# Attention steps of a hybrid decoder moved by one or two products between the matrix products

## The chip, the cores and the metric

The kernel runs on one core of one Trainium2 chip. A core has five engines that run at the same time, each with its own queue that is worked off in order: TensorE (PE in the profile; its weight loads are shown apart as PEld), VectorE (DVE), ScalarE (ACT), GpSimd (POOL) and SyncE (SP), and DMA queues that move data between memory and the on-chip buffers. Engines wait for each other with semaphores. The metric is the time of one execution on the device in microseconds (us).

## The reference

The program computes one inference step of a four-layer decoder, cut here to two layers, on 1024 prompt tokens and 8 decode tokens, all with D_MODEL = 2048, in float32. Layer A mixes by pooling and a gate, then projects out. After it, one shared pair of keys and values is projected. Layer B is sliding-window attention with a learned sink per head:

```python
def attn_core(q, k, v, q_pos, k_pos, sinks):
    s = jnp.einsum('...qkgd,...skd->...kgqs', q, k).astype(jnp.float32) * (HEAD_DIM ** -0.5)
    ...
    s = jnp.where(mask[..., None, None, :, :], s, NEG)
    sink = sinks.astype(jnp.float32).reshape(N_KV_HEADS, GROUP)[:, :, None, None]
    m = jnp.maximum(jnp.max(s, axis=-1, keepdims=True), sink)
    p = jnp.exp(s - m)
    p = p / (jnp.sum(p, axis=-1, keepdims=True) + jnp.exp(sink - m))
    return jnp.einsum('...kgqs,...skd->...qkgd', p.astype(v.dtype), v)
```

Around it stand two large products: `z = x @ w_in` gives queries and gate, and `(o * silu(gate)) @ w_out` goes into a LayerNorm with the residual. There are 32 heads of 64 channels, 4 key heads, and a window of 128 positions.

## The kernel before

**Products.** Nearly all of TensorE's time is large matrix products. The tokens are cut into two chunks of 512 and 520. A product block of 2 by 2 is computed with Strassen's seven products instead of eight (`seven`, `pair`): each of the seven takes one weight block of 128 x 1024, which ScalarE rounds to a high part (`cast_to`, line 475) and VectorE completes by the rest (`prep_to`, line 490), and 24 matmuls of 256 or 260 columns: high times high, high times low, low times high (lines 654 to 656). In this document a *product* is one of these groups of 24 matmuls, and a *slot* is one product with what is issued around it.

**The order of the work** is written out by hand. `begin` opens a slot: it first issues what the product before left over (`flush`), then the loads, casts and subtractions of weights some products ahead. Then come the 24 matmuls. `end` closes the slot: it issues on TensorE what was entered with `self.product(n, rank, go)` for this slot, lower rank first, and then what was entered with `self.at(n, go)` for it; n counts slots from where the entry is made. So everything entered in a slot stands in an engine's queue behind the weight work of that slot and ahead of the left-over work of the next. `in_order` keeps this order on TensorE, VectorE and ScalarE.

**The left-over work of the seven products** moves partial sums between three accumulator banks called a, b, c. The products run in the order 0, 2, 1, 5, 3, 4, 6; I call their places 0 to 6. After place 0 ScalarE writes the negative of bank a into bank b (line 593), and the product at place 2 adds to bank b. After place 2 ScalarE copies bank b out (line 602), before the product at place 4 adds to it. After place 4 ScalarE copies bank b into bank a (line 614), before the product at place 6 adds to it. Lines 599, 608 and 627 are further copies by ScalarE, and lines 615 and 620 subtractions by VectorE.

**The attention stage** (phase `bi`) makes, per pair p of query tiles, seven products for the queries (places 0 to 6, slots 0 to 6) and seven for the gates (slots 7 to 13). When a query pair is done, SyncE moves a rotated copy (line 1612), and VectorE applies the rotary embedding at the end of slot 10 with three large operations (two at line 1620, one at line 1728): the *rope*. Then each of the two query tiles t of the pair goes through the steps of `attend`, entered in slots counted from the start of the pair:

- `score`: TensorE writes scores to the accumulator tile S (line 1758)
- `select`: ScalarE copies the older half of the window (line 1775)
- `largest`: VectorE puts in the newer half and takes the maximum (lines 1779 to 1787)
- `expo(0)`, `expo(1)`: ScalarE exponentials of four heads' blocks each, with sums (lines 1792, 1794)
- `total`: VectorE adds the sink's part and inverts (lines 1801, 1802)
- `norm(0)`, `norm(1)`: ScalarE scales four blocks each (line 1807)
- `turn`: TensorE transposes into the first half of S (line 1811)
- `keep`: ScalarE copies the transposes (line 1820), then VectorE writes a masked copy of them (line 1821)
- `values`: TensorE multiplies by the values (line 1835)
- `gate`: VectorE multiplies by the gate (line 1844); in chunk 0 every second tile adds four sums and differences (lines 822 to 825)

The two tiles of a pair start seven slots apart, so with `at` = 11 + 7n each step always meets the same place of the seven. A gate's tanh (line 1873) follows the last product of the gates. Large buffers come from one set of 53 (`Mem`), and the one that has been free longest is taken next; in phase `bi` of chunk 1 the distance at which weights are prepared drops from 3 to 2 products where fewer than 4 are free. In chunk 0 the first four pairs run as plain products with a different step, and only pairs 4 to 7 run as sevens; there VectorE also makes four sums of weight blocks per seven products (line 333) for chunk 1. Chunk 1 runs all eight pairs as sevens, and in pairs 4 and 7 with steps of the decode tokens in between (`decode`).

Of the kernel before, what the change touches and what calls it, by code (L numbers as in the profile page):

```python
# [74 lines left out]
X_AGE = 3  # L75
SIDE_KEEP = 5

DEC_AT = (0, 1, 6, 6, 7, 8, 9, 10, 13, 13), (11, 11, 12, 12, 13, 14, 15, 16, 17, 17)


# [101 lines left out]
class Kern:  # L182
# [1556 lines left out]
        self.at(0, a)  # L1739
        self.at(lag, b)  # L1740

    def attend(self, c, t, at, s1, s2, late=False):


        nc = self.nc
# [43 lines left out]
        def expo(n):  # L1789
            mx, nm, es, rs = x["sm"]  # L1790
            if n == 0:
                nc.scalar.activation(es[:], es[:], AF.Exp)
            for i in range(4 * n, 4 * n + 4):
                nc.scalar.activation(  # L1794
                    x["s3"][:, i, :], x["s3"][:, i, :], AF.Exp, bias=nm[:, i : i + 1], scale=0.125,
                    accum_out=rs[:, i : i + 1],
                )
# [6 lines left out]
        def norm(n):  # L1804
            rs = x["sm"][3]
            for i in range(4 * n, 4 * n + 4):
                nc.scalar.activation(x["s3"][:, i, :], x["s3"][:, i, :], AF.Copy, scale=rs[:, i : i + 1])
# [48 lines left out]
                z.free()  # L1856

        self.product(at, 2, score)
        for n, go in enumerate((
            select, largest, lambda: expo(0), lambda: expo(1), total, lambda: norm(0), lambda: norm(1)  # L1860
        )):
            self.at(at + 1 + n, go)
        self.product(at + s1, 0, turn)
        self.at(at + s1 + 1, keep)
        self.product(at + s1 + s2, 1, values)
# [32 lines left out]
    def decode(self, c, pr):  # L1898
# [86 lines left out]

        for n, go in zip(DEC_AT[pr], (s0, s1, s2, s3, s4, s5, s6, s7, s8, s9)):
            if go in (s0, s2, s6, s8):
# [6 lines left out]
    def phase_bi(self, c, ps, nxt):  # L1994
        nc = self.nc
        T = CHUNKS[c][1]
        if ps[0] == 0:
            self.kv_open(c)
        if not self.strassen:
            for done in (self.k_done, self.v_done):  # L2000
                box = {}
                for j in range(2):

                    def take(ps, j=j, done=done, box=box):
                        if j == 0:
                            box["s"] = self.mem.full()
                        nc.scalar.copy(box["s"].a[:, j * T : (j + 1) * T], ps[:])
                        if j == 1:
                            done(c, box["s"])

                    self.unit(take)
            for t in range(2 * ps[0], 2 * ps[-1] + 2):
                def q_done(ps, t=t):
                    s = self.mem.half()
                    nc.scalar.copy(s.a[:, :T], ps[:])
                    self.q_done(c, t, s, 1, 4)

                def g_done(ps, t=t):
                    s = self.mem.half()
                    nc.scalar.copy(s.a[:, :T], ps[:])  # L2020
                    self.gate_done(c, t, s, 1)

                self.attend(c, t, 9, 13 if t <= 2 * ps[-1] else 8, 2)
                self.unit(q_done)
                if t == 2 * ps[-1] - 1:
                    self.x_begin(nxt)
                self.last = t == 2 * ps[-1] + 1
                self.unit(g_done)
            self.last = False
            return  # L2030
        if ps[0] == 0:
            pairs = []
            for done in (self.k_done, self.v_done):
                box, z0, z1 = self.two(T)
                pairs.append((z0, z1, lambda done=done, box=box: done(c, box["s"])))
            self.both(c, *pairs)

        def queries(p):
            t0 = 2 * p
            if T > TP and p % 4 == 3:  # L2040
                self.at(2, lambda p=p: self.dec_keys(p // 4))
            for n in range(2):
                t = t0 + n
                self.attend(c, t, 11 + 7 * n, {13: 10, 14: 10, 15: 8}.get(t, 12), 2, t > 12)
            if p == ps[-1]:
                self.x_begin(nxt)
                if c == 1:
                    self.ahead = 6, 3, 2
            box, z0, z1 = self.two(T)
            self.pair(c, z0, z1, lambda t0=t0, box=box: self.q_done(c, t0, box["s"], 2, 3))  # L2050

        def gates(p):
            box, z0, z1 = self.two(T)

            def done():
                self.gate_done(c, 2 * p, box["s"], 2)
                if T > TP and p % 4 == 3:
                    self.decode(c, p // 4)

            self.last = p == ps[-1]  # L2060
            self.pair(c, z0, z1, done)

        for p in ps:
            queries(p)
            gates(p)
        self.last = False
# [260 lines left out]
```

## Time and profile before

| what | value |
|---|---|
| median of 3 runs | 2356.72 us (2354.07 to 2358.65) |
| profiled execution | 2351.39 us |
| its span, first to last instruction | 2349.6 us |
| TensorE busy with matmuls | 2303.9 us, 98% |
| VectorE busy | 1923.6 us, 82% |
| ScalarE busy | 1363.3 us, 58% |
| DMA engines, HBM | 279 GB/s over the span |
| sevens of phase `bi`, chunk 0 | about 1342 to 1540 us of the span |
| sevens of phase `bi`, chunk 1 | about 1540 to 1976 us of the span |

How to read it: matmuls are pipelined, so the 0.28 us of one matmul overlap with the next; what tells about TensorE is where it sat idle and who released it. "A <- B" in a wait means that A's engine sat idle until B was done. A group of instructions is named by its line, engine, operation and the tiles that it writes and reads: `m` are the large buffers, `pD` the accumulator banks of the products, `pS` the tile S, `pO` the bank of `values`.

### The profile page before, as it was taken

How to read it: one execution, taken by the hardware profiler on the slowest of the kernel's cores; microseconds unless marked ns; L12 is line 12 of the kernel's file. 1: busy time of each engine (PE TensorE's matmuls, PEld its weight loads, DVE VectorE, ACT ScalarE, POOL GpSimd, SP SyncE). 2: the span in 40 equal slices, each digit the busy share in tenths (PEclk: the TensorE clock that was granted, in tenths of full speed). 3: DMA queues.
4: the chain of work that ended last, by engine and by line, in shares of the span. 5: the costliest groups of instructions: out<-in, count | busy, mean ns of one | idle time of the engine just before them, and what ended most of it. 6: DMA issues, size and time to landing. Idle time of an engine off the chain costs nothing. (4 is left out here: it accounts for less than half of the span.)

```text
span 2349.6 us, 49653 instructions
## 1 busy us (share of the span) xinstructions
PE 2303.9 (98%) x19960; PEld 2203.0 (94%) x19960; DVE 1923.6 (82%) x2386; ACT 1363.3 (58%) x2502; POOL 201.9 (9%) x379
## 2 busy tenths in 40 slices
PE   8999999999999999999999999999999999999997
PEld 6899999999999999998777899999999999999997
DVE  8788998776878878868998888897777768888887
ACT  4454446544546547554464666685676678556656
POOL 0111110001000000000111111100000000000000
PEclk9999999999999999999999999999999999999999
DMA  8668789989889989999799766688787768699785
GB/s 291 213 242 308 268 294 340 339 280 324 298 289 346 321 283 335 321 330 324 265 329 358 262 220 220 225 312 283 232 256 240 233 195 304 230 352 369 268 302 194
DMA packets 252072, 669.39 MB, mean 285 GB/s; under 512 B 25760, under 2 KB 106560, under 8 KB 251840
## 3 DMA queue, kind: packets, MB, share of 16 engines
q1 hardware_dynamic: 206368, 501.14, 63.6%
q0 software_dynamic: 45472, 165.07, 18.1%
q8 instruction: 156, 2.56, 0.4%
q14 instruction: 76, 0.62, 0.1%
HBM read 471.01 MB, written 185.59 MB: 279 GB/s over the span
## 5 line engine op out<-in xcount | busy, mean ns | idle before, releaser
L654 PE MATMUL pD<-m,m 128*128 128x260 f32 (+1 forms) x4752 | 1346.4, 283 | 11.0 <-ACT pD L593 8.4
L656 PE MATMUL pD<-m,m 128*128 128x260 f32 (+1 forms) x4752 | 1340.1, 282 | 5.7 <-DVE m L490 5.6
L655 PE MATMUL pD<-m,m 128*128 128x260 f32 (+1 forms) x4752 | 1339.8, 282 | 1.1 <-DVE m L774 1.1
L654 PEld LDWEIGHTS pD<-m,m 128*128 128x128 f32 x4752 | 895.1, 188 | 20.5 <-ACT pD L593 9.9
L656 PEld LDWEIGHTS pD<-m,m 128*128 128x128 f32 x4752 | 895.9, 189 | 7.9 <-DVE m L490 7.9
L655 PEld LDWEIGHTS pD<-m,m 128*128 128x128 f32 x4752 | 895.6, 188 | 1.8 <-DVE m L774 1.3
L490 DVE TENSOR_TENSOR m<-m,m 128x1024 fp32r<-128x1024 f32 x674 | 813.6, 1219 | 88.0 <-ACT m L475 57.5
L475 ACT CAST m<-m 128x1024 fp32r<-128x1024 f32 x674 | 703.6, 1048 | 259.1 <-DVE m L333 66.7
L682 PE MATMUL pD<-m,m 128*128 128x512 f32 x448 | 179.5, 401 | 8.1 <-ACT m L765 8.1
L683 PE MATMUL pD<-m,m 128*128 128x512 f32 x448 | 177.1, 395 | 1.0 <-DVE m L774 1.0
L684 PE MATMUL pD<-m,m 128*128 128x512 f32 x448 | 177.0, 395 | 0.0
L774 DVE TENSOR_TENSOR m<-m,m 128x1024 fp32r<-128x1024 f32 (+1 forms) x120 | 146.8, 1225 | 7.2 <-ACT m L765 5.5
L765 ACT CAST m<-m 128x1024 fp32r<-128x1024 f32 (+1 forms) x120 | 125.7, 1052 | 14.4 <-PE pD L683 5.2
L615 DVE TENSOR_TENSOR m<-pD,m 128x260 f32<-128x260 f32 (+1 forms) x86 | 36.5, 424 | 106.9 <-ACT pD L614 99.4
L627 ACT COPY m<-pD 128x260 f32<-128x260 f32 (+1 forms) x83 | 31.0, 373 | 149.9 <-PE pD L656 149.9
L682 PEld LDWEIGHTS pD<-m,m 128*128 128x128 f32 x448 | 84.5, 189 | 29.4 <-ACT m L765 8.1
L333 DVE TENSOR_TENSOR m<-m,m 128x1024 f32<-128x1024 f32 x88 | 107.6, 1222 | 5.1 <-DMA m<-in_wia 3.6
L683 PEld LDWEIGHTS pD<-m,m 128*128 128x128 f32 x448 | 84.6, 189 | 20.9 <-DVE m L774 2.1
L684 PEld LDWEIGHTS pD<-m,m 128*128 128x128 f32 x448 | 84.5, 189 | 19.8
L1794 ACT ACTIVATE m<-m,sm 128x128 f32<-128x128 f32 x256 | 99.2, 389 | 0.0
L1084 PE MATMUL pD<-m,m 128*128 128x260 f32 (+1 forms) x528 | 91.5, 323 | 0.0
L1084 PEld LDWEIGHTS pD<-m,m 128*128 128x128 f32 x528 | 79.5, 188 | 8.2
(245 smaller groups left out, 2113.8 us busy)
## 6 DMA issues: line engine op xcount, KB each, us to landing
m<-in_wia SPq DMA_DIRECT2D x124, 512.0 KB
m<-in_wib SPq DMA_DIRECT2D x120, 512.0 KB
swia<-m POOLq DMA_DIRECT2D x64, 512.0 KB, 4.8
m<-swia SPq DMA_DIRECT2D x64, 512.0 KB
m<-swoa SPq DMA_DIRECT2D x64, 512.0 KB
swib<-m POOLq DMA_DIRECT2D x64, 512.0 KB, 5.1
m<-swib SPq DMA_DIRECT2D x64, 512.0 KB
m<-swob SPq DMA_DIRECT2D x56, 512.0 KB
```

The costliest lines, as they stand in the source:

```text
L333: self.nc.vector.tensor_add(s[out].a[:, :1024], s[x].a[:, :1024], s[y].a[:, :1024])
L475: self.nc.scalar.copy(hi.r[:, :1024], self.stream[self.cast].src().a[:, :1024])
L490: self.nc.vector.tensor_sub(lo.r[:, :1024], s.src().a[:, :1024], hi.a[:, :1024])
L654: nc.tensor.matmul(ps[:, :TH], wh[:, s], h, start=new and k == 0, stop=False, skip_group_check=on)
L655: nc.tensor.matmul(ps[:, :TH], wh[:, s], l, start=False, stop=False, skip_group_check=on)
L656: nc.tensor.matmul(ps[:, :TH], wl[:, s], h, start=False, stop=k == 7, skip_group_check=on)
L682: nc.tensor.matmul(ps[:], wh[:, s], h, start=par == 0 and k == 0, stop=False)
L683: nc.tensor.matmul(ps[:], wh[:, s], l, start=False, stop=False)
L684: nc.tensor.matmul(ps[:], wl[:, s], h, start=False, stop=par == 1 and k == 7)
L765: self.nc.scalar.copy(h.r[:, :n], s.a[:, :n])
L774: self.nc.vector.tensor_sub(l.r[:, :n], s.a[:, :n], h.a[:, :n])
L1084: nc.tensor.matmul(ps[:, : cs.stop - cs.start], ws[:, s], d[:, cs], start=f0 and k == 0, stop=l0 and k == 3,)
```

## The change

For query tiles below 14 in the sevens (tiles 8 to 13 of chunk 0, 0 to 13 of chunk 1) `attend` starts one slot later (12 + 7n instead of 11 + 7n) and follows a second list of steps in which everything from `expo(1)` to `norm(1)` comes one slot later still. `turn`, `keep`, `values` and `gate` come one slot later too, except for tiles 12 and 13, where a smaller `s1` keeps them in the slots they had. Tiles 14 and 15 and the plain pairs are as before. No instruction is added or removed.

| step | place before | place after |
|---|---|---|
| `turn` | 2 | 3 |
| `keep` | 3 | 4 |
| `values`, then `score` of a later tile | 4 | 5 |
| `select` | 5 | 6 |
| `gate` | 5 | 6 |
| `largest` | 6 | 0 |
| `expo(0)` | 0 | 1 |
| `expo(1)` | 1 | 3 |
| `total` | 2 | 4 |
| `norm(0)` | 3 | 5 |
| `norm(1)` | 4 | 6 |

The rope stays at the end of slot 10 (place 3 of the gates), and the casts, subtractions and left-over work of the products stay where they are.

```diff
+CLOSE, SPREAD = (1, 2, 3, 4, 5, 6, 7), (1, 2, 3, 5, 6, 7, 8)
...
-    def attend(self, c, t, at, s1, s2, late=False):
+    def attend(self, c, t, at, s1, s2, late=False, ticks=CLOSE):
...
-        for n, go in enumerate((
+        for n, go in zip(ticks, (
             select, largest, lambda: expo(0), lambda: expo(1), total, lambda: norm(0), lambda: norm(1)
         )):
-            self.at(at + 1 + n, go)
+            self.at(at + n, go)
...
                 t = t0 + n
-                self.attend(c, t, 11 + 7 * n, {13: 10, 14: 10, 15: 8}.get(t, 12), 2, t > 12)
+                at, s1, ticks = (12 + 7 * n, {12: 11, 13: 9}.get(t, 12), SPREAD) if t < 14 else (
+                    11 + 7 * n, {14: 10, 15: 8}[t], CLOSE
+                )
+                self.attend(c, t, at, s1, 2, t > 12, ticks)
```

## The prediction

> **What bounds the kernel now.** I read the page first, then the stage that the change touches, then who ended TensorE's waits there, then single places in order of time. The page: busy time, share, instructions.
>
> ```profile
> PE 2303.9 (98%) x19960; PEld 2203.0 (94%) x19960; DVE 1923.6 (82%) x2386; ACT 1363.3 (58%) x2502; POOL 201.9 (9%) x379
> ```
>
> TensorE is the bound: only its idle time can be won. By stage (length, then busy time per engine; pairs 4 to 7 of chunk 0, start of chunk 1, its pairs):
>
> ```profile
> 1362.00:1540.00 178.00, 171.09 (x1914) 165.73 (x1913) 151.58 (x177) 117.89 (x274) 21.58 (x44) 1.00 0.70 239
> 1540.00:1600.00 60.00, 60.00 (x603) 58.70 (x602) 52.03 (x65) 46.84 (x103) 3.76 (x7) 1.00 0.83 284
> 1600.00:1976.00 376.00, 375.03 (x4159) 366.16 (x4157) 277.88 (x365) 254.65 (x602) 20.10 (x31) 1.00 0.75 242
> ```
>
> So 6.9 us can be won in chunk 0, where VectorE is busy 85%, and 1.0 in chunk 1. TensorE's waits in 1362 to 1976 (total, times, longest):
>
> ```profile
> PE pD L654 <- ACT pD L593: 5.6, 4, 1.9
> PE pS L1758 <- DVE m L1728: 1.6, 1, 1.6
> PE pD L642 <- ACT m L627: 0.5, 1, 0.5
> ```
>
> The third is the start of chunk 1, which the change leaves. The other two are 7.2 us, 0.31% of the profiled time. The worst place of the first, in order of time (start, length, what; in brackets the idle time before):
>
> ```profile
> 1490.18 1.34 DVE L1779 COPY_PREDICATED m<-mki,pS 128x1024 f32<-128x1024 int32 x1
> 1491.56 1.22 DVE L1783 TENSOR_REDUCE sm<-m 128x8 f32<-128x1024 f32 x1
> 1493.02 0.17 DVE L1787 TENSOR_TENSOR sm<-sm,nsink 128x8 f32<-128x8 f32 x1
> ...
> 1489.25 0.37 ACT L627 COPY m<-pD 128x256 f32<-128x256 f32 x1
> 1489.64 1.06 ACT L1873 ACTIVATE m<-m 128x1024 f32<-128x1024 f32 x1
> 1490.61 1.04 ACT L475 CAST m<-m 128x1024 fp32r<-128x1024 f32 x1
> 1493.22 0.21 ACT L1792 ACTIVATE sm<-sm 128x8 f32<-128x8 f32 x1 [1.57 <-DVE sm L1787]
> ...
> 1494.87 0.36 ACT L593 ACTIVATE pD<-pD 128x256 f32<-128x256 f32 x1
> ...
> 1493.14 0.28 PE L656 MATMUL pD<-m,m 128*128 128x256 f32 x1
> 1495.29 0.39 PE L654 MATMUL pD<-m,m 128*128 128x256 f32 x1 [1.87 <-ACT pD L593]
> ```
>
> VectorE is late with `largest`; ScalarE stands idle for it 1.57 us at the head of `expo(0)`, which lasts 1.65 (1493.22 to 1494.87); behind `expo(0)` in the same queue stands line 593, and TensorE cannot begin the product at place 2 before that has filled bank b. The second wait:
>
> ```profile
> 1475.76 1.22 DVE L1821 TENSOR_TENSOR m<-pS,cst 128x1024 f32<-128x1024 f32 x1 [0.90 <-ACT m L1820]
> 1476.90 2.35 DVE L1620 TENSOR_TENSOR m<-m,m 128x1024 f32<-128x1024 f32 x2
> 1479.28 1.22 DVE L1728 TENSOR_TENSOR m<-m,m 128x1024 f32<-128x1024 f32 x1
> ...
> 1480.56 0.63 PE L1758 MATMUL pS<-m,m 64*32 64x160 f32 x22 [1.64 <-DVE m L1728]
> ```
>
> `keep`, held up by ScalarE, stands ahead of the rope, and `score` needs the rope.
>
> **Prices.** One round of seven products with one tile's steps, TensorE's part of it, and the means of 1362 to 1976 (busy, mean ns of one, idle before):
>
> ```profile
> 1498.15:1522.40 24.25, 24.25 (x274) 23.55 (x274) 21.02 (x28) 15.94 (x41) 3.53 (x7) 1.00 0.69 237
> ...
> L1835 PE MATMUL pO<-m,m 128*64 128x128 f32 x32 | 2.0, 276 | 0.0
> L1758 PE MATMUL pS<-m,m 64*32 64x160 f32 x64 | 1.3, 299 | 0.0
> L1811 PE MATMUL pS<-cst,m 128*128 128x128 f32 x8 | 1.0, 272 | 0.0
> ...
> L475 ACT CAST m<-m 128x1024 fp32r<-128x1024 f32 x175 | 183.1, 1047 | 71.2 <-DVE m L490 15.0 <-DVE m L333 13.0 <-PE pD L656 12.6
> L1807 ACT ACTIVATE m<-m,sm 128x128 f32<-128x128 f32 x184 | 59.0, 396 | 0.0
> L1820 ACT COPY m<-pS 128x1024 f32<-128x1024 f32 x23 | 23.3, 1012 | 0.0
> L1775 ACT COPY m<-pS 128x1024 f32<-128x1024 f32 (+1 forms) x23 | 21.6, 938 | 8.9 <-PE pS L1758 6.6 <-DVE m L490 2.1
> ...
> L490 DVE TENSOR_TENSOR m<-m,m 128x1024 fp32r<-128x1024 f32 x175 | 211.9, 1219 | 37.4 <-ACT m L475 18.1 <-PE pD L655 8.7 <-PE pO L1835 3.5
> L333 DVE TENSOR_TENSOR m<-m,m 128x1024 f32<-128x1024 f32 x26 | 31.8, 1223 | 0.5
> L1821 DVE TENSOR_TENSOR m<-pS,cst 128x1024 f32<-128x1024 f32 x23 | 28.2, 1225 | 31.3 <-ACT m L1820 21.9 <-PE pD L655 7.9 <-ACT m L1807 1.5
> L1844 DVE SCALAR_TENSOR_TENSOR m<-pO,m 128x512 f32<-128x512 f32 x20 | 13.7, 684 | 0.0
> L620 DVE TENSOR_TENSOR m<-pD,m 128x260 f32<-128x260 f32 (+1 forms) x25 | 10.6, 424 | 23.5 <-PE pD L656 23.4
> ```
>
> A product lasts (24.25 - 2.0 - 1.3 - 1.0) / 7 = 2.85 us. No instruction comes or goes, so every busy sum stays; only the order in the queues costs or pays.
>
> **VectorE ahead of `expo(0)`, chunk 0.** Before, place 5 holds a subtraction of banks (0.42), one of weights (1.22), two sums of weights (2.45), `gate` (0.68) and on every second tile four more of about 0.42: 6.4 us. Place 6 holds 0.42 + 1.22 + `largest` (1.34 + 1.22 + 2 x 0.17 = 2.90): 4.5. Together 10.9 us of work in two products of 2.85, so `largest` ends 5.2 after place 6 ends. Then `expo(0)` 1.65 and line 593 0.36 make 7.2, against the 5.7 of places 0 and 1: a wait of 1.5 us. The trace has four of 0.9 to 1.9, so the count is sound.
> After, line 593 stands ahead of `expo(0)`. ScalarE's queue from the start of place 6: cast 1.05, `norm(1)` 4 x 0.396 = 1.58, `select` 0.94, line 627 0.37, tanh 1.06, cast 1.05, line 593 0.36: 6.4 us against 3 x 2.85 = 8.55 when it is wanted. The 5.6 us go, with 2.1 to spare. What is late next is `expo(0)` itself: VectorE has 4.1 at place 5, which now lasts 2.85 + 2.0 + 1.3 because `values` and `score` stand there, so it starts place 6 on time; it has 4.0 there and 4.1 at place 0, so `largest` ends 2.4 after place 0; `expo(0)`, line 599 and a cast are done 5.5 after place 0. Line 602 has to wait for the product at place 2 in any case, which ends at 5.7, and it is wanted at 8.55, so nothing of this reaches TensorE. `expo(1)` stands behind 602. Ahead of line 614, where `norm(1)` stood, there is only `keep` with its 1.0.
>
> **`score` behind the rope.** It moves one product, 2.85 us, later and the rope does not: the 1.6 us go.
>
> **`keep` behind the rope: the price that the trace does not show.** Before, `keep` stood ahead of the rope; after, once per pair (pairs 5 and 6 of chunk 0, 1 to 6 of chunk 1), it comes in slot 11, behind the rope of slot 10. Count from T, the end of slot 10's matmuls, where `turn` begins. VectorE can take slot 10's subtraction from T - 2.85 on, since the buffer for its result comes free with the product before: it ends at -1.63, the rope of 3 x 1.22 at 2.03, the next subtraction at 3.25, a weight sum (chunk 0 only) at 4.47, the masked copy at 5.69. `values` wants that at T + 1.0 + 2 x 2.85 = 6.7. So there is a reserve of 1.0 in chunk 0 and 2.2 in chunk 1, and the lower end of this price is nothing. A gain is not in it: `values` has to wait for its products in any case. The upper end comes from the place quoted, the only one where the rope was seen late. There `values` ended at 1480.56 - 1.64 = 1478.92, so slot 10's matmuls ended 2.0 and 2.85 before that, at 1474.07, and the rope began at 1476.90, 2.83 later; 0.90 + 1.22 of that is `keep`, which no longer stands ahead. Left is T + 0.71. From there the masked copy ends at T + 8.0, which is 1.3 too late in chunk 0, and at 6.8 without the weight sum, 0.1 too late in chunk 1: 2 x 1.3 + 6 x 0.1 = 3.2 us. The whole trace has one wait of `values` for the masked copy, the first row here (the second is used for rival C):
>
> ```profile
> PE pS L1835 <- DVE m L1821: 0.6, 1, 0.6
> PE pD L656 <- DVE m L490: 5.6, 10, 1.3
> ```
>
> I take that 0.6, between the ends, at the two tight places of chunk 0: 1.2 us.
>
> The row of line 1821 above says that VectorE idled 21.9 us until ScalarE's copy of line 1820 was done, although both only read S. The Trainium skill, PSUM — Partial Sum Buffer, section "PSUM bank collisions raise a hardware error", says why: ScalarE and VectorE may not be in the same bank at once, reads included, so software has to put one after the other. By that rule the late case would be dearer where the copy's buffer is the one that slot 11's subtraction has just freed, which the built order has at two places of chunk 1: subtraction 5.6, copy 6.6, masked copy 7.8 instead of 6.8, so 3.2 + 2 x 1.0 = 5.2 us. The idle row agrees with the rule.
>
> **The rest.** Tiles 12 and 13 keep `turn`, so the ends of both chunks keep their order; `norm(0)` and `norm(1)` of tile 13 (2 x 1.58) come into the last two slots; line 627 there waits for the last matmuls anyway (the 0.5 row), so nothing. Two decode steps now meet `gate` in their slot and have to wait until it has read their bank; `gate` can start at the end of `values`, a product earlier: nothing. POOL's stores of `gate` and a memset move one slot with their tiles, behind no new producer; readers come in the next phase. SyncE gets no step; its weight loads shift a slot where a buffer becomes free later.
>
> Sum: -5.6 - 1.6 + 1.2 = -6.0 us. On the profiled 2351.39 (1.8 around the span) that is 2345.4; the median shown is 5.3 higher, so 2350.7. Within 0.2% (4.7 us) is about what a measurement cannot tell from no change.
>
> **Rivals.** A: `keep` behind the rope gives back its upper end, 3.2: 2356.7 - 7.2 + 3.2 = 2352.7, a gain of less than 0.2%; it decides from 2.5 us on. For it speaks VectorE's 85% in chunk 0; against it that only two places are tight. By the rule on the banks it would give 2354.7.
> B: the waits only change places, because VectorE's lateness stays and `expo(0)` still blocks ScalarE, now ahead of lines 599 and 602: 2356.7. Against it: 602 has 2.5 us in hand.
> C, slower: buffers. Query and gate tiles stay in use one product longer in chunk 1, where free ones are few; the weight distance drops to 2 in 28 slots instead of 25, and TensorE waits for line 490, as in the second row above (ten times, at most 1.3). To be slower by 4.7 it has to eat 7.2 too: nine waits of 1.3. Twelve would give 2356.7 - 7.2 + 15.6 = 2365. Against it: chunk 1 shows 1.0 us of idle, none for line 490.
>
> **Chances.** Forecast 0.56, A 0.24, B 0.08, C 0.12. A and B are no change: faster 0.56, same 0.32, slower 0.12. Predicted 2350.7. The range goes from the full 7.2 and the runs' own spread below the median (2.6) to A and B: 2347 to 2357; the likeliest alone is 2348 to 2352.
>
> **What would show it.** In 1362 to 1540 TensorE's idle falls from 6.9 to under 2, and line 593 and line 1728 leave its waits. Line 593 stands ahead of line 1792, and ScalarE may still idle for line 1787. If A holds, "L1835 <- L1821" appears, up to eight times; if B, line 602 as releaser; if C, line 490 between 1600 and 1976. The prediction is wrong if the waits go and the time does not.

## The result, and the profile after

After the change the median is 2345.61 us (2344.57 to 2346.48, 5 runs), against 2354.16 us (2354.04 to 2358.65, 5 runs) for the kernel before beside it: a ratio of 0.9964, 95% interval 0.9953 to 0.9975, so 8.5 us faster (5.9 to 11.1). The forecast was faster by 6.0, at 2350.7, within 2347 to 2357. The direction was right and the 6.0 lies inside the interval, but the time measured is 1.4 us below the range. In the kernel after and in those derived from it all lines named here have a number one higher than before.

The profiled execution after took 2344.57 us, 6.8 less than before's 2351.39. Its page, first part:

```profile
PE 2302.7 (98%) x19960; PEld 2202.7 (94%) x19960; DVE 1923.7 (82%) x2386; ACT 1365.4 (58%) x2502; POOL 202.3 (9%) x379
```

The 6.8 by stretches, first before, then after. Each stretch ends where TensorE goes on after a wait that both kernels have (the second wait at the start of pair 4 of chunk 0, the start of chunk 1, the start of the last stage). The columns are: from and to, length, then busy time and count for PE, PEld, DVE, ACT and POOL, granted clock, DMA share, GB/s.

```profile
0.00:1357.49 1357.49, 1339.39 (x10241) 1261.17 (x10241) 1118.71 (x1403) 711.03 (x1144) 132.99 (x257) 1.00 0.86 302
1357.49:1538.59 181.10, 174.19 (x1928) 168.85 (x1928) 154.71 (x178) 117.92 (x281) 22.00 (x44) 0.99 0.68 235
1538.59:1976.43 437.84, 436.44 (x4767) 426.24 (x4768) 331.69 (x432) 303.30 (x707) 23.86 (x38) 1.00 0.76 248
1976.43:2349.60 373.17, 353.87 (x3025) 346.72 (x3025) 318.52 (x376) 231.00 (x373) 23.04 (x40) 0.99 0.83 291
```

```profile
0.00:1356.85 1356.85, 1339.22 (x10241) 1261.27 (x10241) 1118.87 (x1403) 711.59 (x1144) 133.39 (x257) 1.00 0.86 302
1356.85:1532.54 175.69, 173.19 (x1928) 168.76 (x1928) 154.33 (x177) 119.37 (x281) 22.08 (x44) 0.99 0.71 246
1532.54:1971.11 438.57, 436.63 (x4767) 426.04 (x4768) 331.71 (x433) 303.84 (x707) 23.91 (x38) 1.00 0.75 247
1971.11:2342.80 371.69, 353.63 (x3025) 346.65 (x3025) 318.77 (x376) 230.58 (x373) 22.95 (x40) 0.99 0.82 291
```

Chunk 0 is 5.4 us shorter and chunk 1 is 0.7 longer, so the stage that was changed gave 4.7. The last stage, which the change does not touch, gave 1.5, and the stretch ahead of the change, untouched as well, 0.6. What TensorE still waited for from 1362 to 1976 (total, times, longest):

```profile
PE pS L1759 <- DVE m L1729: 1.3, 1, 1.3
PE pD L643 <- ACT m L628: 1.2, 1, 1.2
PE pD L657 <- DVE m L491: 1.0, 1, 1.0
PE pD L655 <- ACT m L628: 0.5, 1, 0.5
PE pO L1836 <- DVE m L1822: 0.4, 1, 0.4
```

The four waits for line 593 (now 594) are gone, and so is the one of `score` at 1480. ScalarE in order of time, chunk 0, shows why:

```profile
1508.88 0.37 ACT L594 ACTIVATE pD<-pD 128x256 f32<-128x256 f32 x1 [1.38 <-PE pD L657]
...
1510.86 0.21 ACT L1793 ACTIVATE sm<-sm 128x8 f32<-128x8 f32 x1 [0.66 <-DVE sm L1788]
```

Ahead of line 594 ScalarE now idles only for TensorE. ScalarE still stands idle for `largest` (line 1788), but behind the hand-over of bank b, where nobody wants it.

Three waits are new or longer. The first is `score` of tile 14 in pair 7, in order of time, ScalarE and then VectorE and TensorE:

```profile
1515.85 0.37 ACT L600 COPY m<-pD 128x256 f32<-128x256 f32 x1 [3.24 <-DMA to<-m]
...
1518.28 1.02 ACT L1821 COPY m<-pS 128x1024 f32<-128x1024 f32 x1
...
1519.34 1.22 DVE L1822 TENSOR_TENSOR m<-pS,cst 128x1024 f32<-128x1024 f32 x1 [0.91 <-ACT m L1821]
1520.48 2.35 DVE L1621 TENSOR_TENSOR m<-m,m 128x1024 f32<-128x1024 f32 x2
1522.87 1.23 DVE L1729 TENSOR_TENSOR m<-m,m 128x1024 f32<-128x1024 f32 x1
...
1524.15 0.74 PE L1759 MATMUL pS<-m,m 64*32 64x160 f32 x27 [1.28 <-DVE m L1729]
```

Tile 12 keeps its `turn` and `keep`, so here `keep` still stands ahead of the rope, and tile 14's scores keep their slot too. ScalarE stood 3.24 us before line 600 because the buffer that it writes was still being stored by a DMA; so `keep` was late, then the rope, then the scores. The second is the start of chunk 1, ScalarE:

```profile
1526.22 1.27 ACT L1808 ACTIVATE m<-m,sm 128x128 f32<-128x128 f32 x4
...
1529.99 1.28 ACT L1808 ACTIVATE m<-m,sm 128x128 f32<-128x128 f32 x4
...
1532.12 0.37 ACT L628 COPY m<-pD 128x256 f32<-128x256 f32 x1
```

ScalarE runs without a gap up to line 628: the two norms of tile 13, 1.27 and 1.28, came in ahead of it. The wait grew from 0.46 to 1.21 us. The third is a decode step in pair 4 of chunk 1 (TensorE, VectorE, TensorE):

```profile
1773.84 1.26 PE L1930 MATMUL pS<-qd,m 64*128 64x8 f32 x20
...
1775.22 1.34 DVE L1780 COPY_PREDICATED m<-mki,pS 128x1024 f32<-128x1024 int32 x1 [5.80 <-PE pS L1930]
...
1779.41 0.39 PE L657 MATMUL pD<-m,m 128*128 128x260 f32 x1 [1.02 <-DVE m L491]
```

Before, `largest` of tile 6 stood in the last slot of pair 3. It now stands in the first of pair 4, behind `s0` of the decode step, whose scores go to other columns of S but to the same banks; VectorE idled 5.80 us, until line 1930 was done, and TensorE then waited 1.02 for a prepared weight (line 491).

### The profile page after: what moved, and what is told of

It is laid out like the page before. It is cut to its first block, busy times and chain, and to the rows that moved or that the text cites. A ratio compares the mean times of both kernels' runs of the same rounds, so it can differ in the third digit from the quotient of the medians.

```text
span 2342.8 us, 49652 instructions
## 1 busy us (share of the span) xinstructions
PE 2302.7 (98%) x19960; PEld 2202.7 (94%) x19960; DVE 1923.7 (82%) x2386; ACT 1365.4 (58%) x2502; POOL 202.3 (9%) x379
## 5 line engine op out<-in xcount | busy, mean ns | idle before, releaser
L655 PEld LDWEIGHTS pD<-m,m 128*128 128x128 f32 x4752 | 895.5, 188 | 13.2 <-issue 5.1
L657 PEld LDWEIGHTS pD<-m,m 128*128 128x128 f32 x4752 | 895.9, 189 | 8.5 <-DVE m L491 8.5
L656 PEld LDWEIGHTS pD<-m,m 128*128 128x128 f32 x4752 | 895.5, 188 | 1.8 <-DVE m L775 1.3
L683 PEld LDWEIGHTS pD<-m,m 128*128 128x128 f32 x448 | 84.6, 189 | 29.5 <-ACT m L766 8.1
L684 PEld LDWEIGHTS pD<-m,m 128*128 128x128 f32 x448 | 84.6, 189 | 20.8 <-DVE m L775 2.1
L685 PEld LDWEIGHTS pD<-m,m 128*128 128x128 f32 x448 | 84.5, 189 | 19.7
L1795 ACT ACTIVATE m<-m,sm 128x128 f32<-128x128 f32 x256 | 99.2, 391 | 0.0
L1808 ACT ACTIVATE m<-m,sm 128x128 f32<-128x128 f32 x256 | 81.9, 392 | 12.8 <-DVE sm L1803 12.8
```

The lines of the kernel that those rows point to most:

```text
L655: nc.tensor.matmul(ps[:, :TH], wh[:, s], h, start=new and k == 0, stop=False, skip_group_check=on)
L656: nc.tensor.matmul(ps[:, :TH], wh[:, s], l, start=False, stop=False, skip_group_check=on)
L657: nc.tensor.matmul(ps[:, :TH], wl[:, s], h, start=False, stop=k == 7, skip_group_check=on)
L683: nc.tensor.matmul(ps[:], wh[:, s], h, start=par == 0 and k == 0, stop=False)
L684: nc.tensor.matmul(ps[:], wh[:, s], l, start=False, stop=False)
L685: nc.tensor.matmul(ps[:], wl[:, s], h, start=False, stop=par == 1 and k == 7)
```

## The experiments

Two theories were to be told apart for the waits that went. Q: the order of ScalarE's queue made them (line 593 behind `expo(0)`). V: VectorE's lateness makes them, and they only change their place (rival B on record). A third question came up with the table above: whether the last stage gained by the change or by chance (S and N in the expectations).

**before_again**: no edit. **after_again**: no edit.

> The kernel before, unchanged, once more. If the 8.5 us between the medians are the change alone, its profile shows the same waits of TensorE in 1362 to 1976 as the first one (line 593 5.6, line 1728 1.6) and a ratio of 1.000. If a part of them is how much one execution differs from the next, its profiled span lies some 2 to 3 us above the first one's 2349.6, and the excess has to stand in waits or in a stage that the change does not touch.

> The changed kernel, once more. If the first measurement was right: 8.5 us faster than before (5.9 to 11.1). If the forecast's sum of 6.0 was right and the rest was spread: 5 to 7 us.

Before again: 2351.97 us, ratio 0.9992 (0.9984 to 1.0001). After again: 2347.18 us, ratio 0.9974 (0.9963 to 0.9984), so 6.1 us faster (3.8 to 8.7), which is the 6.0 of the forecast; the two measurements of the change, 8.5 and 6.1, agree within their intervals. The profiles repeat the waits of their kernels: for line 593 four times, 5.6 us in all; after, 1.7, 1.5, 1.0, 0.5 and 0.4. The wait of `score` at 1480 is 0.8 in the repeat instead of 1.6.

**exp_late**: the second half of the softmax later, but `score`, `turn`, `keep`, `values` in their old slots.

```diff
-CLOSE, SPREAD = (1, 2, 3, 4, 5, 6, 7), (1, 2, 3, 5, 6, 7, 8)
+CLOSE, SPREAD = (1, 2, 3, 4, 5, 6, 7), (1, 2, 4, 6, 7, 8, 9)
...
-                at, s1, ticks = (12 + 7 * n, {12: 11, 13: 9}.get(t, 12), SPREAD) if t < 14 else (
+                at, s1, ticks = (11 + 7 * n, {13: 10}.get(t, 12), SPREAD) if t < 14 else (
```

> Only the exponentials, the total and the two scalings go to the slots of the changed kernel; scores, select, largest, turn, keep, values and gate stay where they were. Theory Q (what costs is expo(0) ahead of line 593 in ScalarE's queue): the four waits for line 593 go, the wait of score for the rope (1.6) stays, the crowding by tile 13's scalings at the end of chunk 0 (0.7) comes: 5.6 - 0.7 = 4.9 us faster. Theory V (the gain is VectorE's, by spreading keep, rope, gate and largest over other slots): no gain, within 1 us of before, and the waits for line 593 are still there.

2344.48 us, ratio 0.9962 (0.9949 to 0.9974). TensorE's waits from 1362 to 1976, whole:

```profile
PE pD L643 <- ACT m L628: 1.7, 1, 1.7
PE pS L1759 <- DVE m L1729: 0.5, 1, 0.5
PE pD L655 <- ACT m L628: 0.5, 1, 0.5
```

No wait for line 594 is left though VectorE has the same work in the same places up to `largest`. That speaks for Q, and this part alone brings as much as the whole change (8.9 us, where 4.9 were expected).

One thing was expected otherwise: the wait of `score` at 1480 is gone too, though `score`, rope and `keep` have the slots of before (the 0.5 is another place, at 1716.98). ScalarE's copy of `keep`, before and then in exp_late, and `score` in exp_late:

```profile
1474.72 1.00 ACT L1820 COPY m<-pS 128x1024 f32<-128x1024 f32 x1
...
1470.55 1.02 ACT L1821 COPY m<-pS 128x1024 f32<-128x1024 f32 x1
...
1477.82 1.32 PE L1759 MATMUL pS<-m,m 64*32 64x160 f32 x64
```

Before, this copy stood behind `expo(1)` and behind a cast that had idled 2.59 us, at 1469.80, for a store of `to`. In exp_late `expo(1)` comes after it and ScalarE does not idle for that store there, so the rope is done when `score` comes. Which of the two took the wait away was not tried.

**exp_ahead**: the kernel after, with `expo(0)` back in the slot of `largest`, ahead of line 594; all else as after.

```diff
-CLOSE, SPREAD = (1, 2, 3, 4, 5, 6, 7), (1, 2, 3, 5, 6, 7, 8)
+CLOSE, SPREAD = (1, 2, 3, 4, 5, 6, 7), (1, 2, 2, 5, 6, 7, 8)
```

> The changed kernel with expo(0) alone put back ahead of line 593 (in the slot of largest). Theory Q: VectorE ends largest 2.4 us after place 0 on the tiles with the four extra sums and about 1.0 on the others, then 1.65 and 0.36, against 2.85: 1.6 or 0.2 us of wait on each of 20 tiles, about 3 x 1.6 + 17 x 0.3 = 10 us slower than the changed kernel, with line 593 as the releaser. Theory V: no difference from the changed kernel.

2361.82 us, ratio 1.0036 (1.0023 to 1.0048): 14.6 us slower than after beside it (10 expected), and slower than before. One step per tile moved by one slot, and the wait is back, twelve times:

```profile
PE pD L655 <- ACT pD L594: 12.8, 12, 2.2
```

Q holds. Since `expo(0)` stands here in the slot that it had before, this is also the rest of the change by itself: it is a loss, since `largest` then is later and line 594 still behind it.

**chunk0_only, chunk1_only, chunk0_again**: the change for one chunk; the other has before's slots.

```diff
-                at, s1, ticks = (12 + 7 * n, {12: 11, 13: 9}.get(t, 12), SPREAD) if t < 14 else (
-                    11 + 7 * n, {14: 10, 15: 8}[t], CLOSE
+                at, s1, ticks = (12 + 7 * n, {12: 11, 13: 9}.get(t, 12), SPREAD) if t < 14 and c == 0 else (
+                    11 + 7 * n, {13: 10, 14: 10, 15: 8}.get(t, 12), CLOSE
```

> The changed order for the tiles of chunk 0 alone; chunk 1 as before. The account by stages (theory S): chunk 0 loses its waits for lines 593 and 1728 (4.8 + 1.6 = 6.4 us in the profile of before) and gains the wait of score for the rope at pair 7 (1.3) and the longer start of chunk 1 (0.7); chunk 1 keeps its one wait for line 593 (0.9). That is -4.4 us against before, and the profile from 1362 to 1976 shows just these waits. The last stage tells where the further 1.7 us come from: if the changed order of buffers out of chunk 0 removes the wait for line 615 near 2130, the kernel is 6.1 us faster than before; if chunk 1 does it, the wait of about 1.6 is still there and the gain is 4.4. Theory N (the last stage has nothing to do with the change): the wait is there in one run and not in the next, whichever part is changed.

> The changed order for the tiles of chunk 1 alone. Theory S: the wait for line 593 at chunk 1 (0.9) goes, the waits for the late weights behind the decode step (1.0) and for keep behind the rope (0.4) come; chunk 0 keeps its 6.4: +0.5 us against before, no measurable change, or a loss. If chunk 1's order is what removes the last stage's wait for line 615 (1.6), the sum is -1.1 instead. The prediction on record had a gain in chunk 1 too (0.9 less nothing). A gain of more than 2 us would refute the account by stages.

> chunk0_only once more, one profile. If its wait of 5.9 us for line 491 near 2121 belongs to the kernel (the order in which buffers come free), it is there again, between 4 and 8 us. If it was an accident of one execution, the place shows the wait of 1.2 to 1.9 for line 615, or none, and the span is some 4 us shorter than 2348.6.

Chunk 0 alone: 2351.84 us, ratio 0.9994 (0.9985 to 1.0003). Chunk 1 alone: 2350.88 us, 0.9992 (0.9984 to 1.0001). Neither is measurably different from before, while both together bring 0.26 to 0.36%. The waits in the stage are at the places that the account by stages said. The three largest, for chunk 0 alone (2.5 where 1.2 was expected):

```profile
PE pD L643 <- ACT m L628: 2.5, 1, 2.5
PE pS L1759 <- DVE m L1729: 0.9, 1, 0.9
PE pD L655 <- ACT pD L594: 0.8, 1, 0.8
```

and for chunk 1 alone:

```profile
PE pD L655 <- ACT pD L594: 4.8, 3, 1.9
PE pS L1759 <- DVE m L1729: 1.0, 1, 1.0
PE pD L657 <- DVE m L491: 1.0, 1, 1.0
```

What chunk 0 alone wins (from 1358.38 to 1971.11 are 612.7 us, before 618.9) it loses for the most part in the last stage (377.5 us, before 373.2), where neither expectation had it. The repeat shows it again (all waits after 1976, first line):

```profile
PE pD L657 <- DVE m L491: 9.4, 6, 6.6
```

In chunk0_only the same wait is 5.9 us, at 2120.69. VectorE there:

```profile
2116.79 0.43 DVE L823 TENSOR_TENSOR m<-m 128x260 f32<-128x260 f32 x1 [6.14 <-DMA m<-o]
```

A load of `o` came late and held up all that VectorE had behind it. So N falls: what the last stage waits for repeats with the kernel. In the profiles where `score`, rope and `keep` of chunk 1 keep their old order (before, before_again, exp_late, and both profiles of exp_late_13 below) there is a wait of 1.2 to 1.9 us for line 614 or 615 near 2130; in those with the new order in chunk 1 (after, after_again, exp_ahead, chunk1_only and the mended ones below) there is none. Chunk 0 alone is the exception: it keeps the old order in chunk 1, and has the wait for line 491 in place of the one for line 615. So chunk 0's order counts as well. ScalarE around it, before:

```profile
2131.07 1.04 ACT L475 CAST m<-m 128x1024 fp32r<-128x1024 f32 x1 [1.98 <-DMA m<-in_wob]
2132.02 0.37 ACT L614 COPY pD<-pD 128x256 f32<-128x256 f32 x1
```

and after:

```profile
2124.61 1.05 ACT L476 CAST m<-m 128x1024 fp32r<-128x1024 f32 x1 [0.75 <-DMA m<-in_wob]
2125.56 0.37 ACT L615 COPY pD<-pD 128x256 f32<-128x256 f32 x1
```

The cast ahead of the hand-over waits for a weight load. SyncE issues the loads, and a load into a buffer has to wait until the store that last read it is done. In SyncE's queue between 2060 and 2140 one such wait, for a store of `to`, is 7.8 us before:

```profile
SPq L274 <- DMA to<-m: 7.8, 1, 7.8
```

after, 3.2:

```profile
SPq L275 <- DMA to<-m: 3.2, 1, 3.2
```

The longest wait for this store is 6.6 to 7.8 us in the five profiles that have the wait near 2130, and at most 3.2 in the seven with the new order in chunk 1. Waits for other stores do not go with it: after_again has one of 7.6 for `swob` and no wait near 2130. Buffers are handed out by how long they have been free, so a new order can change which buffer the last stage's loads get; that it comes about in this way is argued, since the buffers were not traced.

**mended**: after, with the first two decode steps one slot later and tile 13's softmax at the old distances.

```diff
-DEC_AT = (0, 1, 6, 6, 7, 8, 9, 10, 13, 13), (11, 11, 12, 12, 13, 14, 15, 16, 17, 17)
+DEC_AT = (1, 2, 6, 6, 7, 8, 9, 10, 13, 13), (11, 11, 12, 12, 13, 14, 15, 16, 17, 17)
...
-                at, s1, ticks = (12 + 7 * n, {12: 11, 13: 9}.get(t, 12), SPREAD) if t < 14 else (
+                at, s1, ticks = (12 + 7 * n, {12: 11, 13: 9}.get(t, 12), CLOSE if t == 13 else SPREAD) if t < 14 else (
```

> After with two of its new waits taken away: the first two decode steps a slot later (so that the one in pair 4 of chunk 1 no longer stands ahead of the masked copy and the largest of a query tile), and tile 13 with its exponential and norms at the old distances. If the decode step is what delays VectorE and the two norms what delays line 628, the wait for line 491 near 1780 (1.0) goes and the wait for line 628 at the start of chunk 1 falls from 1.2-1.7 to 0.5: about 1.7 to 2.2 us faster than after, 8 to 8.5 faster than before. Rival: VectorE's work is only pushed on, and the same waits turn up one product later or at other lines; then no difference to after, or a wait for line 594 at tile 13 comes back (0.9 to 1.9), since its exponential stands ahead of that line again.

2345.28 us, ratio 0.9969 (0.9958 to 0.9981): no measurable difference to after. Both causes are borne out, the wait for line 491 is gone and that for line 628 is 0.5; but in chunk 0 two others have taken their place:

```profile
PE pS L1759 <- DVE m L1729: 2.1, 1, 2.1
PE pD L655 <- ACT m L603: 1.1, 1, 1.1
```

Tile 13's `expo(1)` is back ahead of line 603 and of `keep`, in the place where ScalarE has already lost 3.5 us to the store of pair 7. The rival held for tile 13, not for the decode step.

**exp_late_13, exp_late_13_again**: exp_late, but with tile 13 entirely as before.

```diff
-                at, s1, ticks = (11 + 7 * n, {13: 10}.get(t, 12), SPREAD) if t < 14 else (
+                at, s1, ticks = (11 + 7 * n, {13: 10}.get(t, 12), CLOSE if t == 13 else SPREAD) if t < 14 else (
```

> Only the exponential, the total and the norms later (scores, rope and keep where they were), and this for tiles 0 to 12 alone; tile 13 is as before. Against exp_late_only that differs in tile 13: the start of chunk 1 should wait 0.5 for line 628 instead of 1.7, and everything else be as there: 6.0 + 1.2 = 7.2 us faster than before by the stages (a ratio of 0.9969), 1.2 faster than the kernel with all tiles. Rival: the wait at the start of chunk 1 belongs to the last matmuls of chunk 0, not to the norms; then it stays at 1.2 to 1.7. Tile 13's exponential ahead of line 594 may also bring back one wait of 0.9 to 1.9 there.

> The kernel exp_late_13 once more. Its profile should show the same waits: none between 1362 and 1976 but the 0.5 at the start of chunk 1, and the one for line 615 near 2125 (1.7). The ratio to before should come out at 0.996 within 0.001. What may differ is how often TensorE runs a stretch of 3 us at half its rate after a wait: 0 to 3 times in the profiles so far, 1.6 us each.

2344.24 us, ratio 0.9959 (0.9945 to 0.9972), and again 2343.28 us, 0.9958 (0.9944 to 0.9971). From 1362 to 1976 both profiles have only the two waits of 0.5 that end a chunk:

```profile
PE pD L655 <- ACT m L628: 0.5, 1, 0.5
PE pD L643 <- ACT m L628: 0.5, 1, 0.5
```

Tile 13 is all that differs from exp_late, so the longer wait at the start of chunk 1 came from its late steps, and the two norms are those seen ahead of line 628. Of the waits between the ends of this stage TensorE has none left.

**both_mended, both_mended_2**: chunk 0 as exp_late_13, chunk 1 as mended (a third list of slots, hence line numbers two higher than before), with mended's decode slots. The last two lines of the diff are in the second kernel alone. In the first, tile 13 of chunk 1 has its scores one slot too early, where they overwrite S before `keep` of tile 11 has read it; its instructions are the same, so its time can be read.

```diff
+WIDE = 1, 2, 4, 6, 7, 8, 9
...
+                at, s1, ticks = 11 + 7 * n, {13: 10, 14: 10, 15: 8}.get(t, 12), CLOSE
+                if t < 13:
+                    at, s1, ticks = (at, 12, WIDE) if c == 0 else (at + 1, 11 if t == 12 else 12, SPREAD)
+                elif t == 13 and c == 1:
+                    at, s1 = at + 1, 9
```

> Chunk 0 with only the exponential, total and norms later, tile 13 as before; chunk 1 with the whole change, and the first two decode steps a slot later. The profiles say: chunk 0 and the start of chunk 1 then have one wait of 0.5, chunk 1 one of 0.3 for keep behind the rope. Last stage: the wait for line 615 near 2130 (1.2 to 1.9) stood in the four profiles where chunk 1's score, rope and keep keep their old slots, and in none where they are later. If that order is what decides, the wait is gone here and the kernel is 1.4 us faster than exp_late_13 (0.3 more, 1.7 less), 7.3 + 1.4 = 8.7 us faster than before by its waits, a ratio near 0.9955. If chunk 0's order matters as well (with chunk 0 alone changed, the last stage had one wait of 5.9 for line 491 instead), some wait of 1.5 to 6 turns up there and the kernel is not faster than exp_late_13.

> As both_mended, with tile 13 of chunk 1 moved with its neighbours (scores one product later, second half as in the kernel called mended). One wait of 0.5 at the start of chunk 1, one of 0.3 to 0.4 for keep behind the rope in chunk 1, none for line 615 near 2125: 1.4 us faster than exp_late_13 by its waits, a ratio to before near 0.9955. Rival: tile 13's exponential, again ahead of a copy of ScalarE, brings back a wait at the last pair of chunk 1 (1 to 2 us), or another order of buffers brings back one in the last stage (1.5 to 6); then no faster than exp_late_13.

2341.70 us, ratio 0.9952 (0.9940 to 0.9965), 1.6 us less than exp_late_13_again on the same chip; and 2342.39 us, 0.9957 (0.9943 to 0.9970). Waits of both_mended_2 from 1362 to 1976:

```profile
PE pD L656 <- ACT m L629: 0.5, 1, 0.5
PE pD L644 <- ACT m L629: 0.5, 1, 0.5
PE pO L1837 <- DVE m L1823: 0.3, 1, 0.3
```

Neither profile has the wait near 2125, and SyncE's wait for a store there is 1.8 us. That is what was expected if chunk 1's order decides, with this order in chunk 0. The profile of both_mended_2 has the least idle TensorE of all that keep the computation (2340.0 - 2302.1 = 37.9 us of its span, against 40.1 after and 45.7 before); by the medians it cannot be told from exp_late_13.

## Why the prediction was wrong, step by step

**What failed: the base.** The step was "the median shown is 5.3 higher, so 2350.7". This term measured 1.0: after's median is 2345.61 and its profiled run 2344.57, where the sum from the trace had given 2345.4. The median of three runs of before was itself too high: beside the later kernels the medians of before were 2354.16, 2353.43, 2352.77, 2353.87 and 2353.24, that is 2.6 to 3.9 lower, and so much of the miss of 5.1 us is the base. The range's lower end took the whole 7.2 of the waits and 2.6 for the spread below that median; a gain outside the changed stage was not in it. That the sum comes so near to the profiled run is in part luck: the stage that the change touches gave 4.7 of the 6.0, and 2.1 came from stretches that it does not touch.

**Lines 593 and 594: right.** All four waits went, in both profiles, by the mechanism told; exp_late and exp_ahead show it from both sides. The size was a little small: each wait costs more than its idle time. TensorE's busy time in chunk 0 is 174.19 before and 171.56 in exp_late_13, which has none of the waits; 1.38 of that is the clock (last section). The other 1.2 I put down to the four waits of chunk 0 (three for line 593, one of `score`), 0.3 each. That fits an estimate from the rows: the first matmul behind the wait at 1495.29 shows 0.39 us, where one in the stream adds 2.85 / 24 = 0.12.

**`score` behind the rope: the wait went, the reason is not shown.** The prediction had the 1.6 go because `score` moves and the rope does not. In exp_late nothing of this moves and the wait goes all the same; in no run does `score` move while `expo(1)` stays. The term of 1.6 held for one execution (0.8 in the repeat), and pair 7 has a new wait of 1.3 to 1.5, where `keep`, held up by ScalarE, again stands ahead of the rope. The prediction took tiles 12 to 14, which keep their slots, as unchanged; their neighbours in ScalarE's queue had changed.

**`keep` behind the rope: 1.2 in chunk 0 expected, 0.4 in chunk 1 measured.** Neither tight place of chunk 0 waited, and Rival A fell. The one wait is in pair 4 of chunk 1 (at 1817.16). The 0.6 by which the term was sized stands in the last stage, at 2030.96, with no rope ahead of it, and is there after the change too (0.7).

**"So nothing": two misses.** The prediction had tile 13's two norms land ahead of line 628 and cost nothing, since line 628 "waits for the last matmuls anyway": it measured 0.7 to 1.2 more in the two profiles of after, and 2.0 in chunk0_only. It listed the decode steps that meet `gate` and overlooked the first one, which now stands ahead of `largest`: 1.0. With these, the changed stage of the profile roughly adds up: in chunk 0, the waits gone -6.4 and what they cost beyond their idle time -1.2, the new waits + 1.3 + 0.7 and 0.2 for the clock make the -5.4 measured; chunk 1 -0.9 + 1.0 + 0.4 is +0.5 of the +0.7.

**SyncE: "its weight loads shift a slot", costed at nothing.** It is worth 1.5 us in the last stage, in this kernel's favour by luck; with chunk 0 alone the same kind of shift costs 4.3 (377.5 against 373.2 us for the stage).

**Rivals B and C fell.** Line 602 (603) never became a releaser in after, only in mended (1.1); VectorE's lateness is still there and harmless. Line 490 (491) shows once in chunk 1, behind the decode step and not for want of buffers.

## What to carry to other kernels

In an engine that works its queue off in order, what counts is which instruction with a late input stands ahead of one that hands over an accumulator; moving the first behind the second pays, and making its input later while it stays ahead (exp_ahead) costs more than the change could win. For every step that is moved, and for each that is said to stay, look at its new neighbours on each queue: the costs missed here were all at the ends of the pattern (last pair, chunk boundary, decode pair). And a new order in one stage can move the waits of a later, untouched one by microseconds (here -1.5 to +4.3), so when a change is tried in halves, take a profile of the whole.

## What the hardware showed that was not expected

After some waits TensorE runs at half its rate for 3.4 us. The same wait of 1.83 us for line 593 (594) stands in the trace of before and of chunk1_only; what follows differs. Before:

```profile
1443.00:1446.00 3.00, 3.00 (x25) 3.00 (x26) 2.88 (x4) 3.00 (x11) 0.53 (x1) 1.00 0.71 280
```

chunk1_only:

```profile
1444.00:1447.00 3.00, 3.00 (x17) 3.00 (x16) 2.91 (x3) 3.00 (x11) 0.53 (x1) 0.52 0.75 292
```

25 matmuls at a granted clock of 1.00 against 17 at 0.52. The first 31 matmuls of pair 4 in chunk 0, behind two waits of 0.9 and 1.1, take 4.99 us before and 3.61 in exp_late_13:

```profile
1357.49:1362.48 4.99, 4.99 (x31) 4.99 (x32) 4.96 (x6) 1.46 (x9) 0.53 (x1) 0.69 0.29 118
```

```profile
1359.77:1363.38 3.61, 3.61 (x31) 3.61 (x32) 3.61 (x4) 1.45 (x8) 0.00 (x0) 1.00 0.40 159
```

Such a stretch costs 1.4 to 1.5 us (4.99, or 5.15 in after, against 3.61), and ahead of the last 30 us of the span the profiles here have none to three, in different places for one kernel (after at 1357, after_again at 362 and 1536). The Trainium skill, TensorE: Matmul & The Clock Gate, section "Part 1: The HAM clock gate (the "warmup" mystery)", describes a gate that halves the clock after an idle window of about 3.4 us, counted from a point that the kernel does not set. The half rate, its length and its change from one execution to the next agree; the idle time does not, as single waits of 1.7 and 1.8 us were enough here; past the start of the span only chunk 0 alone had a longer wait than 3.4 (5.9 and 6.6 us), with such a stretch behind it.

The clock records of the traces show what decides between two equal waits. Within a trace the stretches begin whole multiples of 3.41 us apart (before: 1357.17 and 2336.80, 287 x 3.413). Cut into windows of this length, the fourteen profiles have, from 20 to 2320 us, at least 1.66 us of idle TensorE in each window that 3.41 us at half the clock follow, and at most 1.61 in all others but two (1.70 and 1.83). The wait of 1.83 us lies wholly in one window in chunk1_only; before, a window ends at 1442.5 and leaves 1.34 of it on one side. So it is idle time of about half a window that counts here, and where the windows fall is chance.

A kernel with fewer waits of over a microsecond has fewer chances for such a stretch; whether that is why before's runs lie higher above its profile than after's was not tested.
